# Hybrid DeltaNet/S5 trunk on one core: S5 output products batched by block over the four column groups, states rotated in place, weight ring of four in layer 0

## The chip, the core and the metric

The kernel runs on one core of a Trainium2 chip. A core has TensorE (PE, the matrix array; its weight loads are listed apart as PEld), VectorE (DVE), ScalarE (ACT), GpSimd (POOL) and SyncE (SP), whose queue issues nearly all transfers here. Each engine works through its own queue in order and waits on semaphores for the others. The metric is device time in microseconds of one execution; the median of three runs is used.

## The reference, cut to what matters

The trunk has two layers over 256 tokens of width 1024, all in fp32. Layer 0 is a gated DeltaNet (4 heads) beside an S5 state-space part (32 groups of 16 channels with 64 complex states each), one output projection for both, then a dense SwiGLU. Layer 1 is a differential attention and a top-2-of-8 expert SwiGLU. The change touches the S5 part of layer 0:

```python
_, _, xr, xi = lax.associative_scan(combine, (a_r, a_i, bu_r, bu_i), axis=1)
y = (jnp.einsum('gcn,blgn->blgc', c_re.astype(f32), xr) - jnp.einsum('gcn,blgn->blgc', c_im.astype(f32), xi)
     + d_skip.astype(f32).reshape(S5_GROUPS, S5_GROUP) * u32)
...
ga, gb = jnp.split(y @ glu_w.astype(f32) + glu_b.astype(f32), 2, axis=-1)
```

Each complex state is multiplied by a constant a at every token and takes in bu. The output of a group is the real part of C times the state, plus a skip term.

## The kernel before, in words

**S5.** Two groups (2 x 64 = 128 states) fill the 128 partitions and are called a pair. There are 16 pairs in four blocks of four; a block's outputs are 4 x 32 = 128 channels. `s5_steps` goes through the blocks b and the pairs i. For a pair, two matmuls form bu (L1100). VectorE turns it by tables of cosine and sine, so that the complex recurrence becomes two real scans: products with cos (L1108, tile s5a) and sin (L1109, tile s5b), a sum and a difference in place (L1110, L1111), and two scans over the 256 tokens into z (L1113, tile s5c). The states are then turned back: z times cos on VectorE into a new s5a buffer (L1116) and z times sin on GpSimd into a new s5b buffer (L1117). Four matmuls of 32 columns (L1121) form the pair's 32 outputs in its own 32 partitions of a PSUM bank, py, which is held through the block. After the fourth pair VectorE adds the skip term and writes the outputs over uT (L1123). Each fp32 matmul appears in the profile as two weight loads and two matmuls. s5a, s5b and s5c have two buffers each, in the pool s5tmp. The tables of blocks 0 and 1 are made early by `s5_tables`, those of blocks 2 and 3 inside `s5_steps`; they use s5a and s5b buffers too.

**What sets the order.** `weave` merges four generators by a start and a step for each: the input projection with its convolution (`w_in_steps`), the S5 steps, two DeltaNet lanes (`gdn_steps`), and the sums of the adaLN modulation (`ada`). A program scheduler then orders each engine's queue from this order and its own estimate of times. After the weave come `s5_glu`, which needs all four blocks, and `out_proj`, whose first passes take the S5 halves and the first DeltaNet heads, and whose last pass takes the heads of the second lane.

**Weights.** All large weights come in 1 MB tiles through `raw` (L110): each load waits until a buffer of the ring is free, and the loads stand in one queue on SP. `split` cuts a tile into a high part (L131, ScalarE) and a low part (L132, VectorE), since most products are made of three fp32r matmuls. The ada sums in layer 0 are fp32 matmuls with 32 columns that go over the four column groups in turn (L272). The ring has five buffers in layer 0 (rawp); from the feed-forward on, four more (rawp2) join it, nine in all.

**PSUM.** The tag "ms" has two banks; in the weave they hold bu and py. The tag "gd" has four, for DeltaNet.

Of the kernel before, what the change touches and what calls it, by code (L numbers as in the profile page):

```python
# [9 lines left out]
F32 = mybir.dt.float32  # L10
# [3 lines left out]
ALU = mybir.AluOpType  # L14
# [3 lines left out]
P = 128  # L18
T = 256
# [55 lines left out]
class Trunk:  # L75
# [5 lines left out]
    NM = 2  # L81
    OSP = (0, 1, 2, 3)
    S5B = 2
    WB = 1
    U = (6, 7)

# [74 lines left out]
    def build(self, upto=99):  # L161
        tc, nc, a = self.tc, self.nc, self.a
        ctx = ExitStack()
        with ctx:
            ent = ctx.enter_context
            self.RAW = 2048
            self.WN = 1024
            cpool = ent(tc.tile_pool(name="const", bufs=1))
            self.cp = cpool
            self.sm = ent(tc.tile_pool(name="small", bufs=1))  # L170
            self.wp = ent(tc.tile_pool(name="wsplit", bufs=2))
            self.rawp = ent(tc.tile_pool(name="rawp", bufs=5))
            self.psum = ent(tc.tile_pool(name="psum", bufs=2, space=PSUM))
            self.raws, self.wps = [self.rawp], [self.wp]
            with ExitStack() as c2:
                self.even_layer(upto, c2.enter_context)
            if upto < 4:
                return
            self.wp2 = ent(tc.tile_pool(name="wsplit2", bufs=2))
            self.rawp2 = ent(tc.tile_pool(name="rawp2", bufs=4))  # L180
            self.raws = [self.rawp] * 5 + [self.rawp2] * 4
            self.wps = [self.wp] * 2 + [self.wp2] * 2
            with tc.tile_pool(name="ffn", bufs=1) as self.fp:
                self.scr = self.fp
                self.dense_ffn()
            self.debug("x0", self.x, lambda d: d.rearrange("(t p) n -> p t n", p=P))
            if upto < 5:
                return
            with tc.tile_pool(name="att", bufs=1) as self.ap_:
                self.scr = self.ap_  # L190
                self.diff_attention()
            self.debug("xm1", self.x, lambda d: d.rearrange("(t p) n -> p t n", p=P))
            if upto < 6:
                return
            with tc.tile_pool(name="moe", bufs=1) as self.mp, tc.tile_pool(name="rawp3", bufs=self.R3) as rawp3:
                self.scr = self.mp
                self.raws, self.nraw = self.raws + [rawp3] * self.R3, 0
                self.moe()
# [211 lines left out]
    def even_layer(self, upto, ent):  # L410
        tc, nc, a = self.tc, self.nc, self.a
# [9 lines left out]
        with tc.tile_pool(name="early", bufs=1) as self.prep:  # L421
# [34 lines left out]
            for k2 in range(KD // 2):  # L456
# [3 lines left out]
                with self.behind(self.lastada[:1] if k2 == 2 else ()):  # L460
                    for k in (2 * k2, 2 * k2 + 1):
                        for tt in range(NT):
                            nc.tensor.matmul(pba[:, tt * 8:tt * 8 + 8], hF[:, k, tt * P:(tt + 1) * P], wba[:, k, :],
                                             start=(k == 0 and tt == 0), stop=(k == KD - 1 and tt == 1))
                    for b in range(4):
                        out = pu[b // 2][:, (b % 2) * T:(b % 2 + 1) * T]
                        for kk in range(2):
                            k, o = 2 * k2 + kk, slice(512 * kk + b * P, 512 * kk + b * P + P)
# [7 lines left out]
            with self.behind(self.lastsplit + self.later + [mm.ins]):  # L476
                self.gdn_gates(pba)
        self.gd = ent(tc.tile_pool(name="gdn", bufs=2, reuse_waits="tile"))
        self.yTa = None
        self.qkv = {}  # L480

# [187 lines left out]
    def s5_tables(self, b):  # L669

        nc, V, G = self.nc, self.nc.vector, self.nc.gpsimd
# [2 lines left out]
        cosT = self.tab.tile([P, 4, T], F32, tag="cos", name=self.nm("cos"))  # L674
        sinT = self.tab.tile([P, 4, T], F32, tag="sin", name=self.nm("sin"))
        for h in range(2):
            u = self.tmp.tile([P, 2, T], F32, tag="s5a", name=self.nm("tu"))
            n = self.tmp.tile([P, 2, T], F32, tag="s5b", name=self.nm("tn"))
            for i in range(2):
                r = 4 * b + 2 * h + i  # L680
# [6 lines left out]
            n = self.tmp.tile([P, 2, T], F32, tag="s5b", name=self.nm("tn"))  # L687
# [4 lines left out]
            n = self.tmp.tile([P, 2, T], F32, tag="s5b", name=self.nm("tn"))  # L692
# [392 lines left out]
    def s5_steps(self):  # L1085

        nc, ev, tmp = self.nc, self.ev, self.tmp
        V, G = nc.vector, nc.gpsimd
        crT, ncrT, nciT = self.cT
        for b in range(4):  # L1090
            if b >= 2:
                self.s5_tables(b)
            py = None
            for i in range(4):
                self.mark("s5")
                pr, o = 4 * b + i, 32 * i
# [4 lines left out]
                                     self.uT[o:o + 32, b, :], start=True, stop=True)  # L1101
                pb = pb.rearrange("p (k t) -> p k t", t=T)

                def t2(tag):
                    return tmp.tile([P, 2, T], F32, tag=tag, name=self.nm(tag))

                tcs, tsn, z = t2("s5a"), t2("s5b"), t2("s5c")
                V.tensor_tensor(tcs, pb, cosv, op=ALU.mult)  # L1108
                V.tensor_tensor(tsn, pb, sinv, op=ALU.mult)  # L1109
                V.tensor_tensor(tcs[:, 0, :], tcs[:, 0, :], tsn[:, 1, :], op=ALU.add)  # L1110
# [1 line left out]
                for kind in range(2):  # L1112
                    V.tensor_tensor_scan(z[:, kind, :], self.mag[:, pr:pr + 1].to_broadcast([P, T]), tcs[:, kind, :], 0.0,  # L1113
                                         op0=ALU.mult, op1=ALU.add)
                oc, os_ = t2("s5a"), t2("s5b")
                V.tensor_tensor(oc, z, cosv, op=ALU.mult)  # L1116
                (G if i in self.OSP else V).tensor_tensor(os_, z, sinv, op=ALU.mult)  # L1117
                if py is None:
                    py = self.ps("ms", "py")
                for n, (m, x) in enumerate(((crT, oc[:, 0, :]), (ncrT, os_[:, 1, :]), (nciT, os_[:, 0, :]), (nciT, oc[:, 1, :]))):  # L1120
                    nc.tensor.matmul(py[o:o + 32, :T], m[:, b, o:o + 32], x, start=(n == 0), stop=(n == 3))  # L1121
                yield
            V.scalar_tensor_tensor(self.uT[:, b, :], self.uT[:, b, :], self.colB[:, 48 + b:49 + b], py[:, :T],  # L1123
                                   op0=ALU.mult, op1=ALU.add)


    def dense_ffn(self):
# [709 lines left out]
```

## Time and profile before

| what | value |
|---|---|
| median of three runs | 1378.49 us (1377.51 to 1380.19) |
| the profiled execution | 1378.09 us |
| its span, first to last instruction | 1376.3 us |
| granted TensorE clock, mean | 0.978 |
| S5 steps on VectorE, first to last | 78.9 to 235.2 us |

A row of the busy time by stage gives the stretch, its length, the busy time and instruction count of each engine, the granted clock, the share of time that the DMA engines were busy, and GB/s. With a tile or a line chosen, it counts the instructions of that tile or line alone. A row of waits reads: who waited for whom, microseconds in total, how often, the longest. A row of a group ends in: busy us, mean ns of one, idle time of the engine before them and what ended it. A row of the timeline begins with start and length in microseconds; "x4" is four like instructions merged.

### The profile page before, as it was taken

The numbers are of one execution on the slowest core, as the hardware profiler recorded it, in microseconds if no ns is written. First come the engines' busy times: TensorE is split into PE (matmuls) and PEld (weight loads), VectorE is DVE, ScalarE is ACT, GpSimd is POOL, SyncE is SP. The second block draws the span as 40 slices with busy tenths as digits, with TensorE's granted clock in tenths as the row PEclk, the third lists the DMA queues.
The fourth block names the chain that finished last, engine by engine and source line by source line (L and its number), as shares of the span: only waits on it lengthen the run. The fifth ranks groups of instructions, "written<-read, shape, count | busy, mean of one in ns | idle before, by whom it ended". The sixth has DMA issues, their size and how long they took to land.

```text
span 1376.3 us, 26749 instructions
## 1 busy us (share of the span) xinstructions
PE 1281.9 (93%) x10928; PEld 941.8 (68%) x10928; DVE 826.4 (60%) x1516; ACT 577.1 (42%) x990; POOL 123.6 (9%) x118
## 2 busy tenths in 40 slices
PE   3999999989999978999999999999998899999975
PEld 2777666779999978998788435786352468835334
DVE  6688767567878878965798413986020089820202
ACT  3553322455444444664778213775010168711000
POOL 3132322000000003341100000000000000000000
PEclk9799999999999999999999999999999999999998
DMA  9834334159788967821899899999999999999995
GB/s 262 268 114 132 111 106 154 62 177 325 247 270 287 293 211 252 271 96 63 334 305 399 305 380 409 405 409 356 391 409 405 408 409 406 409 397 408 408 396 208
DMA packets 196164, 400.98 MB, mean 291 GB/s; under 512 B 14797, under 2 KB 115650, under 8 KB 196034
## 3 DMA queue, kind: packets, MB, share of 16 engines
q1 hardware_dynamic: 189610, 398.00, 78.7%
q10 hardware_dynamic: 6424, 1.19, 0.5%
q8 instruction: 88, 1.44, 0.4%
q14 instruction: 42, 0.34, 0.1%
HBM read 398.11 MB, written 1.05 MB: 290 GB/s over the span
## 4 chain that ended last, share of the span: by engine, by line
PE 46%; DMA 10%; DVE 4%; issue 1%; ACT 1%; SPq 1%; POOL 0%; ACTq 0%; DVEq 0%
PE pab L1731 9%; DMA raw<-in_odd_expert_w 9%; PE py L1782 5%; PE pab L1675 4%; PE pab L1674 4%; PE pab L1676 4%; PE py L1708 2%; PE py L1709 2%; PE py L1707 2%; PE px L1625 2%; DVE wlo L132 1%; PE pqk L398 1%; PE pqk L399 1%; PE pqk L400 1%; PE pth L150 1%
## 5 line engine op out<-in xcount | busy, mean ns | idle before, releaser
L131 ACT ACTIVATE whi<-raw 128x1024 fp32r<-128x1024 f32 (+2 forms) x352 | 347.1, 1001 | 279.8 <-PE pab L399 52.3
L132 DVE TENSOR_TENSOR wlo<-raw,whi 128x1024 fp32r<-128x1024 f32 (+2 forms) x352 | 402.9, 1168 | 72.6 <-ACT whi L131 70.6
L1731 PE MATMUL pab<-raw,xg 128*32 128x512 f32 (+1 forms) x1920 | 194.2, 524 | 10.5 <-DMA raw<-in_odd_expert_w 10.5
L1731 PEld LDWEIGHTS pab<-raw,xg 128*32 128x32 f32 x1920 | 58.2, 109 | 118.8 <-issue 77.5
L1751 DVE TENSOR_TENSOR hb<-hb,pab 128x256 f32<-128x256 f32 (+1 forms) x35 | 12.4, 364 | 171.0 <-ACT hb L1750 170.5
L1675 PE MATMUL pab<-wlo,xg 128*128 128x512 f32 (+1 forms) x288 | 110.3, 383 | 3.6 <-DVE wlo L132 3.4
L1676 PE MATMUL pab<-whi,xg 128*128 128x512 f32 (+1 forms) x288 | 106.4, 377 | 0.0
L398 PE MATMUL pab<-hT,whi 128*128 128x256 f32 x352 | 101.9, 290 | 0.0
L399 PE MATMUL pab<-hT,whi 128*128 128x256 f32 x352 | 100.3, 285 | 0.1
L400 PE MATMUL pab<-hT,wlo 128*128 128x256 f32 x352 | 99.9, 284 | 0.0
L1782 PE MATMUL py<-raw,hTe 128*32 128x256 f32 (+1 forms) x1760 | 83.7, 343 | 10.7 <-DMA raw<-in_odd_expert_w 8.6
L282 DVE SCALAR_TENSOR_TENSOR adas<-raw,condr,adas 128x256 f32<-128x256 f32 x175 | 86.4, 499 | 3.1
L1674 PE MATMUL pab<-whi,xg 128*128 128x512 f32 (+1 forms) x288 | 84.4, 379 | 3.6 <-DVE xg L1632 1.9
L1782 PEld LDWEIGHTS py<-raw,hTe 128*32 128x32 f32 x1760 | 53.4, 112 | 38.0 <-DMA raw<-in_odd_expert_w 12.8
L1802 DVE TENSOR_TENSOR yf<-py,gate 32x256 f32<-32x256 f32 (+1 forms) x48 | 18.0, 374 | 102.3 <-PE py L1782 101.3
L1750 ACT ACTIVATE hb<-pab 128x256 f32<-128x256 f32 (+1 forms) x35 | 11.5, 338 | 155.8 <-PE pab L1731 155.1
L399 PEld LDWEIGHTS pab<-hT,whi 128*128 128x128 f32 x352 | 68.0, 193 | 0.8 <-DVE hT L388 0.5
L398 PEld LDWEIGHTS pab<-hT,whi 128*128 128x128 f32 x352 | 68.1, 193 | 0.3
L400 PEld LDWEIGHTS pab<-hT,wlo 128*128 128x128 f32 x352 | 67.9, 193 | 0.1
L1675 PEld LDWEIGHTS pab<-wlo,xg 128*128 128x128 f32 x288 | 54.3, 189 | 19.4 <-DVE wlo L132 6.3
L1676 PEld LDWEIGHTS pab<-whi,xg 128*128 128x128 f32 x288 | 54.4, 189 | 10.0
L1674 PEld LDWEIGHTS pab<-whi,xg 128*128 128x128 f32 x288 | 51.0, 189 | 13.7 <-ACT whi L131 2.2
(465 smaller groups left out, 2504.4 us busy)
## 6 DMA issues: line engine op xcount, KB each, us to landing
raw<-in_odd_expert_w SPq DMA_DIRECT2D x215, 1024.0 KB
raw<-in_ada_w SPq DMA_DIRECT2D x48, 1024.0 KB
raw<-in_odd_expert_w SPq DMA_DIRECT2D x64, 768.0 KB
raw<-in_even_ffn_w SPq DMA_DIRECT2D x33, 1024.0 KB
raw<-in_odd_w_qkv SPq DMA_DIRECT2D x12, 1024.0 KB
raw<-in_even_w_in SPq DMA_DIRECT2D x10, 1024.0 KB
raw<-in_even_w_out SPq DMA_DIRECT2D x4, 1024.0 KB
raw<-in_odd_w_out SPq DMA_DIRECT2D x4, 1024.0 KB
```

What stands on the lines that cost most here:

```text
L131: act = nc.scalar.activation(hs, src, AF.Copy)
L132: dve = nc.vector.tensor_tensor(l, src, hs, op=ALU.subtract)
L282: nc.vector.scalar_tensor_tensor(s, w[:, k, :], self.condr[:, k, 0:1], s, op0=ALU.mult, op1=ALU.add)
L398: nc.tensor.matmul(out, wh[:, o:o + P], hT[:, k, 0, :], start=(k == 0), stop=False)
L399: nc.tensor.matmul(out, wh[:, o:o + P], hT[:, k, 1, :], start=False, stop=False)
L400: nc.tensor.matmul(out, wl[:, o:o + P], hT[:, k, 0, :], start=False, stop=(k == kd - 1))
L1625: PE.matmul(px[:, kk * n:kk * n + n], self.xn[:, tt, k * P:(k + 1) * P], Pt[:, tt, :n], start=(tt == 0), stop=(tt == 1))
L1674: PE.matmul(p[:, :m], xg[:, k, 0, :], wh[:, s], start=(k == 0), stop=False)
L1675: PE.matmul(p[:, :m], xg[:, k, 0, :], wl[:, s], start=False, stop=False)
L1676: PE.matmul(p[:, :m], xg[:, k, 1, :], wh[:, s], start=False, stop=(k == KD - 1))
L1731: PE.matmul(pu[t][32 * g:32 * g + 32], xg[:, k, 32 * t:32 * t + 32], v[:, :, g * n:(g + 1) * n], start=(k == 0 and (t == 0 or n > P)), sto ...
L1782: PE.matmul(py[32 * g:32 * g + 32, t], hs[f][t], v[:, i, g * n:(g + 1) * n], start=(f == 0 and t == 0), stop=(f == NF - 1 and t == 1))
```

## The change

The four pairs of a block are first all scanned and rotated back; then 16 matmuls form the block's outputs together, product by product, and within a product pair by pair, so that successive matmuls go to the four column groups in turn. The bank py is taken only then. The rotated states stay in place: z times cos overwrites the pair's s5a buffer, z times sin overwrites z. s5a (five buffers) and s5c (four) move to a new pool, s5out, opened after the early pool is closed; s5b keeps its two. The tables of blocks 0 and 1 get buffers of their own in the early pool. The weight ring has four buffers in layer 0, and five join it afterwards, nine in all as before.

```diff
+    S5O = (5, 4)
...
-            self.rawp = ent(tc.tile_pool(name="rawp", bufs=5))
+            self.rawp = ent(tc.tile_pool(name="rawp", bufs=4))
...
-            self.rawp2 = ent(tc.tile_pool(name="rawp2", bufs=4))
-            self.raws = [self.rawp] * 5 + [self.rawp2] * 4
+            self.rawp2 = ent(tc.tile_pool(name="rawp2", bufs=5))
+            self.raws = [self.rawp] * 4 + [self.rawp2] * 5
...
+        self.s5o = ent(tc.tile_pool(name="s5out", bufs=1))
...
-            u = self.tmp.tile([P, 2, T], F32, tag="s5a", name=self.nm("tu"))
+            if b < 2:
+                u = self.prep.tile([P, 2, T], F32, tag="tu", name=self.nm("tu"), bufs=2)
+            else:
+                u = self.s5o.tile([P, 2, T], F32, tag="s5a", name=self.nm("tu"), bufs=self.S5O[0])
...
-            py = None
+            outs = []
...
-                tcs, tsn, z = t2("s5a"), t2("s5b"), t2("s5c")
+                tcs, tsn, z = t2("s5a", self.s5o, self.S5O[0]), t2("s5b", tmp, 2), t2("s5c", self.s5o, self.S5O[1])
...
-                oc, os_ = t2("s5a"), t2("s5b")
-                V.tensor_tensor(oc, z, cosv, op=ALU.mult)
-                (G if i in self.OSP else V).tensor_tensor(os_, z, sinv, op=ALU.mult)
-                if py is None:
-                    py = self.ps("ms", "py")
-                for n, (m, x) in enumerate(((crT, oc[:, 0, :]), (ncrT, os_[:, 1, :]), (nciT, os_[:, 0, :]), (nciT, oc[:, 1, :]))):
-                    nc.tensor.matmul(py[o:o + 32, :T], m[:, b, o:o + 32], x, start=(n == 0), stop=(n == 3))
-                yield
+
+                V.tensor_tensor(tcs, z, cosv, op=ALU.mult)
+                (G if i in self.OSP else V).tensor_tensor(z, z, sinv, op=ALU.mult)
+                outs.append((tcs, z))
+                if i < 3:
+                    yield
+
+            py = self.ps("ms", "py")
+            for n, (m, k, x) in enumerate(((crT, 0, 0), (ncrT, 1, 1), (nciT, 1, 0), (nciT, 0, 1))):
+                for i in range(4):
+                    o = 32 * i
+                    nc.tensor.matmul(py[o:o + 32, :T], m[:, b, o:o + 32], outs[i][k][:, x, :], start=(n == 0), stop=(n == 3))
             V.scalar_tensor_tensor(self.uT[:, b, :], self.uT[:, b, :], self.colB[:, 48 + b:49 + b], py[:, :T],
                                    op0=ALU.mult, op1=ALU.add)
+            yield
```

More of the change, by code (lines that the diff above doesn't have):

```diff
@@ L1102, in s5_steps, with t2 @@
                 pb = pb.rearrange("p (k t) -> p k t", t=T)
-                def t2(tag):
-                    return tmp.tile([P, 2, T], F32, tag=tag, name=self.nm(tag))
-                tcs, tsn, z = t2("s5a"), t2("s5b"), t2("s5c")
+                def t2(tag, pool, bufs):
+                    return pool.tile([P, 2, T], F32, tag=tag, name=self.nm(tag), bufs=bufs)
+                tcs, tsn, z = t2("s5a", self.s5o, self.S5O[0]), t2("s5b", tmp, 2), t2("s5c", self.s5o, self.S5O[1])
                 V.tensor_tensor(tcs, pb, cosv, op=ALU.mult)
```

## The prediction

> **What bounds the kernel now.** I read the page, then the busy time by stage, then the waits of the stage that holds the S5 work.
>
> ```profile
> span 1376.3 us, 26749 instructions
> PE 1281.9 (93%) x10928; PEld 941.8 (68%) x10928; DVE 826.4 (60%) x1516; ACT 577.1 (42%) x990; POOL 123.6 (9%) x118
> ```
>
> ```profile
> core 0: us, PE busy (x) PEld busy (x) DVE busy (x) ACT busy (x) POOL busy (x), PEclk, DMA share, GB/s
> 75.00:237.00 162.00, 158.59 (x1414) 112.64 (x1412) 126.73 (x251) 54.91 (x111) 44.89 (x36) 0.98 0.38 125
> 237.00:300.00 63.00, 58.99 (x456) 49.64 (x456) 34.38 (x74) 26.11 (x64) 2.67 (x4) 1.00 0.22 74
> ```
>
> The edited code runs in the first of these stretches, 75 to 237 us, where four lanes are woven together. TensorE shows 158.6 of 162 us busy, VectorE 126.7 (78%), and the DMA engines 0.38 of their time. The second stretch (GLU, rest of the DeltaNet lanes, output projection) has TensorE at 59.0 of 63. So time taken off TensorE up to 237 us has work behind it to pull forward, as far as about 300 us. A busy TensorE row alone proves little, since ends of matmuls are modelled; the waits say the same:
>
> ```profile
> PE py L1121 <- DVE s5a L1116: 1.1, 1, 1.1
> PE prow L897 <- POOL rn L158: 0.9, 1, 0.9
> PE pqkv L398 <- DVE cacc L840: 0.7, 1, 0.7
> PE gvb L297 <- ACT adas L277: 0.6, 1, 0.6
> ```
>
> ```profile
> DVE s5a L1116 <- PE py L1121: 6.5, 4, 2.1
> DVE uT L1123 <- PE py L1121: 6.5, 4, 2.5
> DVE s5a L1108 <- PE bu L1100: 3.9, 4, 2.4
> ```
>
> The first four rows are all that TensorE's matmuls waited for in the stretch: 3.3 us. VectorE waits for TensorE, 17 us in these three rows alone. TensorE is the bound here.
>
> **The change, part by part.** *The output matmuls (L1121).* Each pair's output is four fp32 products with 32 output columns, recorded as eight matmuls in one column group. The kernel has a second user of the same shape, the ada matmuls of L272, which are issued over the four column groups in turn, as the new batch will be:
>
> ```profile
> L1121 PE MATMUL py<-s5b,ncT 128*32 128x256 f32 x64 | 17.6, 400 | 0.0
> L272 PE MATMUL gv<-raw,condr 128*32 128x256 f32 x192 | 17.3, 390 | 0.0
> ```
>
> ```profile
> 75.00:237.00 162.00, 34.28 (x128) 12.08 (x128) 1.92 (x4) 0.98 0.38 125
> 75.00:237.00 162.00, 17.34 (x192) 6.08 (x192) 0.98 0.38 125
> ```
>
> ```profile
> 123.06 1.07 PE L272 MATMUL gv<-raw,condr 128*32 128x256 f32 x16
> 124.06 1.13 PE L1100 MATMUL bu<-uT,wb 32*128 32x256 f32 x4
> ```
>
> The second fence is the busy time of the tile py (128 matmuls, 34.28 us) and of L272 (192 matmuls, 17.34 us). One record lasts the same in both (400 and 390 ns), but a py record costs 34.28/128 = 268 ns of TensorE and an ada record 17.34/192 = 90 ns, because four of them run side by side. At the ada price the new 128 records cost 128 x 0.090 = 11.6 us, so 34.28 - 11.56 = 22.7 us go. The batches are twice as long (32 records, the ada ones 16), and 16 records take 124.06 - 123.06 = 1.00 us until the next work starts; with one closing tail of about 0.34 us a batch of 32 would take 2.0 + 0.34 = 2.34 us, four of them 9.4 us, so at most 24.9 us go. I take 22.7.
>
> ```profile
> L272 PEld LDWEIGHTS gv<-raw,condr x192: 105/109/178, 123.1 to 225.8; 128*32 128x32 f32 x192
> ```
>
> A rule speaks against this. The Trainium skill, "TensorE: Matmul & The Clock Gate", Part 3, "The mechanism", says that a weight load overlaps matmuls in flight only where the row group differs; column groups share their row group. By it a batch could not hide its 32 loads and the gain would be near 0 instead of 22.7 us. The trace disagrees: the 192 loads of L272 are 109 ns each, 20.9 us in sum, and occupy 6.08 us of the row above. I keep the row.
>
> *The rotated states in place (L1116, L1117).* Instruction counts and sizes on VectorE and GpSimd do not change. Two orders do. VectorE no longer needs a fresh s5a buffer for z*cos, so its 6.5 us of waiting for py (L1116, above) go. GpSimd now writes z where VectorE has just read it, so its product starts after L1116 and not beside it.
>
> ```profile
> L1116 DVE TENSOR_TENSOR s5a<-s5c,cos 128x512 f32<-128x512 f32 x16 | 15.1, 946 | 7.0 <-PE py L1121 6.5
> L1108 DVE TENSOR_TENSOR s5a<-bu,cos 128x512 f32<-128x512 f32 x16 | 10.9, 684 | 4.0 <-PE bu L1100 3.9
> L1109 DVE TENSOR_TENSOR s5b<-bu,sin 128x512 f32<-128x512 f32 x16 | 10.9, 680 | 0.0
> L1110 DVE TENSOR_TENSOR s5a<-s5a,s5b 128x256 f32<-128x256 f32 x16 | 6.8, 428 | 0.2
> ```
>
> ```profile
> L1117 POOL TENSOR_TENSOR s5b<-s5c,sin 128x512 f32<-128x512 f32 x16 | 24.6, 1536 | 80.2 <-DVE s5c L1113 62.7 <-PE ptr L150 7.3 <-PE gv L272 6.5
> ```
>
> ```profile
> 82.56 1.73 POOL L1117 TENSOR_TENSOR s5b<-s5c,sin 128x512 f32<-128x512 f32 x1 [7.93 <-DVE s5c L1113]
> ```
>
> ```profile
> 83.33 2.04 DVE L132 TENSOR_TENSOR wlo<-raw,whi 128x1024 fp32r<-128x1024 f32 x1 [0.20 <-ACT whi L131]
> 46.72 1.22 DVE L132 TENSOR_TENSOR wlo<-raw,whi 128x1024 fp32r<-128x1024 f32 x1
> ```
>
> L1116 takes 946 ns in the mean where the like-sized L1108 takes 684: it sometimes meets GpSimd. After the change the clash is not gone but lands on whatever VectorE does next; the split at 83.33 us, met by GpSimd's product of 82.56 to 84.29, took 2.04 us where the undisturbed one took 1.22. Bounds: 16 x (946 - 684) = 4.2 us of VectorE time won if no later instruction is hit, and 16 x 0.82 - 4.2 = 8.9 us lost if each product hits a split. I take 0, since clashes occur now at both places.
>
> The Trainium skill, "SBUF — State Buffer", section "SBUF: two separate sides", calls this an exclusive lock between GpSimd and a VectorE operation with two SBUF inputs, the later one waiting out the earlier. The two rows agree: 84.29 + 1.22 is 85.5 us, and the split ended at 85.37. By the rule alone the worst case would be each product blocking VectorE for its whole 1.54 us.
>
> *The join at a block's end.* The batch waits for the fourth pair's GpSimd product, and the next block's first scan needs a z buffer that only the batch frees (four z buffers, four pairs). On VectorE that scan and what is queued behind it (splits, convolution, DeltaNet steps) can stand. The chain is L1116 0.68, then GpSimd 1.54, then the batch 2.34: 4.6 us, of which the next pair's first steps (L1108 and L1109, 1.36 us, and two half-size steps as L1110, 0.86 us) cover 2.2, since a fifth s5a buffer is there. That leaves 2.4 us at each of three joins, 7 us, with other lanes' VectorE and TensorE work to fill it; bounds 0 and 7, I take 3. Tables of blocks 2 and 3 draw on the same five buffers and lie in the same gaps. At the last block 2.34 us of batch replaces 8 x 0.268 = 2.1 us: nothing.
>
> *One matmul bank.* py now occupies one of the two "ms" PSUM buffers for a batch, not for a whole block, so bu of the next pair can run ahead: part of the 3.9 us of L1108. No credit beyond the terms above.
>
> *VectorE nears its own bound.* If the stretch shrinks to 162 - 22.7 = 139.3 us, VectorE's 126.7 us fill 91% of it. The feed-forward stage shows the two side by side that full:
>
> ```profile
> 420.00:440.00 20.00, 20.00 (x148) 19.02 (x147) 17.91 (x34) 7.51 (x10) 0.00 (x0) 1.00 0.92 295
> ```
>
> There VectorE is at 90% and TensorE does not idle. That code is more regular than this stretch; loss between 0 and 8 us, I take 3.
>
> *Ring of four in layer 0, five in the second pool.* Every load of layer 0 goes one freed slot later.
>
> ```profile
> 258.51 0.37 SPq L110 DMA_DIRECT2D raw<-in_even_ffn_w  x1
> ```
>
> ```profile
> 291.45 10.40 SPq L110 DMA_DIRECT2D raw<-in_even_ffn_w  x5
> ```
>
> ```profile
> SPq L110 <- DVE wlo L132: 64.6, 4, 32.5
> ```
>
> ```profile
> 278.48 1.06 ACT L131 ACTIVATE whi<-raw 128x1024 fp32r<-128x1024 f32 x1 [3.98 <-PE po L718]
> ```
>
> ```profile
> 300.41 1.04 ACT L131 ACTIVATE whi<-raw 128x1024 fp32r<-128x1024 f32 x1
> 308.39 1.05 ACT L131 ACTIVATE whi<-raw 128x1024 fp32r<-128x1024 f32 x1
> ```
>
> ```profile
> 300.00:420.00 120.00, 117.37 (x818) 110.85 (x819) 96.74 (x156) 59.72 (x85) 4.87 (x6) 0.97 0.87 292
> ```
>
> The queue of SP does stand for slots here (64.6 us, held by splits). The third output-projection load would go near 257 us and is first split at 278.5: hidden, with 20 us of cover. The first feed-forward load moves from 258.5 to the slot freed at 291.4, and its split stands at 300.4: 9 us of cover for one megabyte, which at 292 GB/s takes 3.6 us. The feed-forward loads behind it come one megabyte, 3.6 us, later; the second split at 308.4 still has its data, and the stage after has DMA at 0.87 with TensorE full. Bounds 0 and 3.6, I take 1.5. Without the cover it would be the whole 3.6. Earlier in the layer there is more cover:
>
> ```profile
> 78.10 22.01 SPq L110 DMA_DIRECT2D raw<-in_ada_w  x3
> ```
>
> These three ada loads go between 78.1 and 100.1 us, and the first of them is read at 123.06 (L272, above), so one slot later, 9 us or so, costs 0. Later stages keep nine buffers: 0.
>
> *New pool.* The pool of s5a and z lies where the early pool was and may wait for its last reader, the gate matmul L809:
>
> ```profile
> L809 PE MATMUL pd<-r,cst x4: 592/592/697, 72.5 to 78.7; 128*128 128x512 f32 x4
> L1108 DVE TENSOR_TENSOR s5a<-bu,cos x16: 677/684/692, 78.9 to 224.8; 128x512 f32<-128x512 f32 x16
> ```
>
> It ends at 78.7 + 0.6 = 79.3, the first S5 step starts at 78.9; 0 or 0.4, I take 0.5 with its wait.
>
> **The sum**, against the profiled execution: 1378.1 - 22.7 + 3 (joins) + 3 (VectorE) + 1.5 (ring) + 0.5 (pool) = 1363.4 us. That execution was timed at 1378.09 us around a span of 1376.3; the median of the runs is 1378.49, 0.4 above, so 1363.8.
>
> **Rivals.** *VectorE takes over as the bound.* With every product hitting a split (+8.9 us) VectorE needs 135.6 us. Of its 162 - 126.7 = 35.3 idle us 17 end with TensorE (the three rows of waits); if the other 18.3 stay, the stretch takes 153.9 us: 8.1 won, 1370.4. For it: 78% already, with chains in every lane. Against: most of its named waits are for TensorE.
>
> *Nothing is won.* The busy row of TensorE hides slack (the weight loads fill only 112.6 of 162 us) and the DeltaNet chain, which also runs to the output projection, sets the end; or the batch does not overlap. Then 1378.5. Against: the four rows of waits, and L272.
>
> *Slower: the join serialises S5.* One block's end costs the whole chain: L1116, GpSimd, a batch queued in order behind other lanes' matmuls (2.5 us, the longest wait for py above), the batch itself, about 7.1 us, four times 28 us, with the tables behind it. If nothing fills this, the stretch grows by 28 - 22.7 = 5 us: 1383.5. It decides from 22.7/4 = 5.7 us of uncovered wait at a join. For it: GDN, S5 and ada were spread by weave steps that fit the old costs. Against: the first steps of the next pair are free of the join, and TensorE has other lanes to run.
>
> **How the numbers follow.** Forecast (8 to 25 us won) 0.70; VectorE 0.10; nothing 0.09; slower 0.11. Low end: the best price without losses, 1378.5 - 24.9 = 1353.6, rounded 1354. High end 1376: it takes in the VectorE rival and leaves out the other two, 0.20. About 0.2%, 2.7 us, is what a measurement can tell from no change; so faster 0.80, same 0.09, slower 0.11.
>
> **What would show it.** Right: py's busy time near 10 to 12 us instead of 34.28; TensorE still over 95% busy in the S5 stretch; the uT update of the last block some 15 us earlier than 234.7; VectorE's waits of L1116 gone.
>
> ```profile
> 234.73 0.48 DVE L1123 SCALAR_TENSOR_TENSOR uT<-uT,colB,py 128x256 f32<-128x256 f32 x1 [1.68 <-PE py L1121]
> ```
>
> Wrong: TensorE rows that wait for s5c products of GpSimd at block ends; VectorE over 95% busy with TensorE idle; a first feed-forward split that waits for its load; or S5 ending early while the output projection still ends near 300 us because DeltaNet does.

## The result, and the profile after

The changed kernel is slower: 1396.14 us (median of four runs, 1393.09 to 1398.92) against 1378.76 (1377.51 to 1380.19, with a fourth run beside the three above), a ratio of 1.0124 with a 95% interval of 1.0098 to 1.0149. That is 17 us lost where 15 won were forecast, and outside the range. The profiled execution took 1397.9 us around a span of 1395.8. Medians here and below are over all executions of a kernel, while ratios leave out slow ones (1828 us at a clock of 0.647 in e1_ring4, 1662 at 0.709 in e11_two, 1405 at 0.950 in e7_half).

The stretch of the edited code, and in it the tile py, in the busy time by stage of the changed kernel (columns as before):

```profile
75.00:237.00 162.00, 142.73 (x1289) 106.71 (x1287) 127.08 (x239) 52.38 (x105) 42.99 (x37) 0.88 0.33 108
```

```profile
75.00:237.00 162.00, 20.07 (x128) 5.66 (x128) 1.89 (x4) 0.88 0.33 108
```

TensorE is busy for 142.7 of the 162 us (158.6 before), VectorE as long as before (127.1 and 126.7), and the granted clock has gone from 0.98 to 0.88. py costs 20.07 us instead of 34.28. So work did leave TensorE, and nothing came forward into the space. TensorE's waits in that stretch, the longest groups:

```profile
PE prow L902 <- POOL rn L159: 5.3, 2, 4.7
PE pkk L918 <- DVE qkvs L904: 3.1, 1, 3.1
PE pqkv L399 <- DVE cacc L845: 3.0, 2, 1.8
PE py L1131 <- DVE s5a L1121: 2.2, 4, 0.7
```

The waits are for DeltaNet's norm (rn), its convolution (cacc) and what follows them (qkvs). The batch itself waits for little (the row of py, and 0.8 us more for GpSimd's products). S5 is not late; its last update of uT starts 4 us earlier than the 234.73 of before:

```profile
230.68 0.48 DVE L1132 SCALAR_TENSOR_TENSOR uT<-uT,colB,py 128x256 f32<-128x256 f32 x1 [2.20 <-PE py L1131]
```

Late is DeltaNet. Its input projections (the last of their three matmul lines; first and last start in us), before and after:

```profile
L400 PE MATMUL pqkv<-hT,wlo x96: 276/282/416, 67.3 to 145.4; 128*128 128x256 f32 x96
```

```profile
L401 PE MATMUL pqkv<-hT,wlo x96: 276/282/416, 67.8 to 158.9; 128*128 128x256 f32 x96
```

They end 13.5 us later. The residual sums at the end of the output projection, before and after, are as late:

```profile
L734 DVE TENSOR_TENSOR x<-x,res x8: 414/422/426, 293.7 to 299.3; 128x256 f32<-128x256 f32 x8
```

```profile
L739 DVE TENSOR_TENSOR x<-x,res x8: 414/416/417, 306.5 to 312.1; 128x256 f32<-128x256 f32 x8
```

So 12.8 us are lost by x. The other 6.7 us between the two profiled executions lie behind it (1376.3 - 299.7 = 1076.6 us from x to the end before, 1083.3 after), in code that the change doesn't touch. Among the variants below this part takes 1075.5 to 1087.0 us and goes with no one edit, so it is not explained here.

**Where the 12.8 us went.** The busy time from 75 us to x, before and after:

```profile
75.00:300.00 225.00, 217.58 (x1870) 162.28 (x1868) 161.12 (x324) 81.02 (x174) 47.55 (x40) 0.98 0.33 110
```

```profile
75.00:313.00 238.00, 213.12 (x1874) 164.49 (x1872) 163.96 (x324) 81.19 (x174) 45.66 (x41) 0.91 0.32 106
```

Each length is idle time, plus busy time lost to a low clock, plus work at full clock. Before: 225 - 217.6 = 7.4 idle, 217.6 x 0.02 = 4.4 lost to the clock, 213.2 of work. After: 24.9 idle, 213.1 x 0.09 = 19.2 lost, 193.9 of work. (The last two are estimates: the clock is given to 0.01, and its mean over the stretch is applied to the busy time. The half-speed stretches themselves, 6.8 us before and 41.0 after, hold 6.7 and 33.1 us of busy time, and half of that is 3.4 and 16.6. So these terms are good to about 3 us.) The work fell by 18 to 19 us, which is near the 22.7 of the forecast. Idle time rose by 17.5, and the clock took 13 to 15 more. 17.5 + 14.8 - 19.3 = 13.0, the difference of the two lengths.

**Where it starts.** VectorE's queue in the first block, before:

```profile
83.33 2.04 DVE L132 TENSOR_TENSOR wlo<-raw,whi 128x1024 fp32r<-128x1024 f32 x1 [0.20 <-ACT whi L131]
85.30 0.99 DVE L840 SCALAR_TENSOR_TENSOR cacc<-pqkv,colB,cacc 128x255 f32<-128x255 f32 x2
86.20 1.21 DVE L132 TENSOR_TENSOR wlo<-raw,whi 128x1024 fp32r<-128x1024 f32 x1
87.33 0.47 DVE L840 SCALAR_TENSOR_TENSOR cacc<-pqkv,colB,cacc 128x253 f32<-128x253 f32 x1
```

and after:

```profile
85.52 0.48 DVE L845 SCALAR_TENSOR_TENSOR cacc<-pqkv,colB,cacc 128x255 f32<-128x255 f32 x1
85.92 0.68 DVE L1113 TENSOR_TENSOR s5a<-bu,cos 128x512 f32<-128x512 f32 x1
86.52 0.68 DVE L1114 TENSOR_TENSOR s5b<-bu,sin 128x512 f32<-128x512 f32 x1
87.11 0.47 DVE L845 SCALAR_TENSOR_TENSOR cacc<-pqkv,colB,cacc 128x254 f32<-128x254 f32 x1
87.50 0.68 DVE L1113 TENSOR_TENSOR s5a<-bu,cos 128x512 f32<-128x512 f32 x1
88.10 0.68 DVE L1114 TENSOR_TENSOR s5b<-bu,sin 128x512 f32<-128x512 f32 x1
...
90.50 0.86 DVE L845 SCALAR_TENSOR_TENSOR cacc<-pqkv,colB,cacc 128x255 f32<-128x255 f32 x2
```

The convolution takes three steps of cacc for each projected tile. Before, they stand together (85.30 to 87.8, with one split between). After, the first products of S5's second and third pair stand between them, and the tile is done at 91.4: 5.8 us instead of 2.5. (The next tile of before is mixed with S5's steps too and takes 3.1 us. Over the whole stretch it is ScalarE's wait for the convolution that tells, 11.6 us before and 36.8 after, in rows further down.) TensorE's next projection waits for the tile:

```profile
91.51 0.55 PE L399 MATMUL pqkv<-hT,whi 128*128 128x256 f32 x1 [1.75 <-DVE cacc L845]
91.86 0.41 PE L400 MATMUL pqkv<-hT,whi 128*128 128x256 f32 x1
```

In the next microseconds the projections' matmuls last 0.41 us where they lasted 0.28. The clock by slices of 3.4 us of the changed kernel shows it:

```profile
85.70:89.10 3.40, 3.18 (x17) 2.23 (x17) 3.40 (x7) 1.21 (x2) 1.27 (x1) 0.99 0.01 2
89.10:92.50 3.40, 1.65 (x7) 1.02 (x5) 3.40 (x8) 0.42 (x1) 0.00 (x0) 0.50 0.39 118
92.50:95.90 3.40, 3.40 (x17) 3.40 (x17) 3.40 (x8) 0.00 (x0) 0.00 (x0) 0.50 0.54 191
```

Two slices run at half clock, the second with TensorE fully busy. VectorE is full in all three, and at 95.9 us the clock is full again. The clock falls at 89.1 us, before the wait of 1.75 us, which begins at 89.8. In the slice ahead of the fall TensorE's rows are busy for 3.18 us, but from 85.5 on with small matmuls alone: S5's input products (32 rows of the array), sums with one column and the first output products (32 columns). Half speed comes six more times before x.

### The profile page after: what moved, and what is told of

Its sections match the earlier page's. It is cut to its first block, busy times and chain, and to the rows that moved or that the text cites. A ratio compares the mean times of both kernels' runs of the same rounds, so it can differ in the third digit from the quotient of the medians.

```text
span 1395.8 us, 26742 instructions
## 1 busy us (share of the span) xinstructions
PE 1280.6 (92%) x10928; PEld 947.1 (68%) x10928; DVE 829.4 (59%) x1516; ACT 578.0 (41%) x990; POOL 119.1 (9%) x118
## 4 chain that ended last, share of the span: by engine, by line
PE 48%; DMA 8%; DVE 4%; issue 1%; ACT 1%; POOL 1%; ACTq 0%; DVEq 0%; POOLq 0%
PE pab L1741 9%; DMA raw<-in_odd_expert_w 7%; PE py L1792 5%; PE pab L1685 4%; PE pab L1684 4%; PE pab L1686 4%; PE py L1718 2%; PE px L1635 2%; PE py L1719 2%; PE py L1717 2%; PE pqk L399 1%; PE pqk L400 1%; DVE yf L1812 1%; PE pqk L401 1%; DVE wlo L133 1%
## 5 line engine op out<-in xcount | busy, mean ns | idle before, releaser
L1685 PEld LDWEIGHTS pab<-wlo,xg 128*128 128x128 f32 x288 | 54.4, 189 | 19.5 <-DVE wlo L133 5.5
```

The source lines that it names most:

```text
L1685: PE.matmul(p[:, :m], xg[:, k, 0, :], wl[:, s], start=False, stop=False)
```

## The experiments

Ratios are to the kernel before on the same chip, with 95% intervals. Different builds of one arithmetic differ by some microseconds through the order that the scheduler finds, and one profiled execution can lie up to 9 us from its kernel's median (e16_conv40: 1388.94 and 1379.90). So verdicts go by ratios, and the profile serves to say where.

**First round: which part of the change.** *e1_ring4*: the kernel before with the weight ring of four and five alone.

> The kernel before with only the weight rings changed (four buffers in layer 0, five after it). Theory A (S5 steps, freed from waiting for TensorE, fill VectorE's queue early, and TensorE idles at 75 to 175 us, with its clock at half after each gap): the ring alone is worth 0 to 3 us, 1378 to 1382. Theory B (later loads are what leaves TensorE without work): most of the 17 us, 1390 or more.

1385.22 us, ratio 1.0038 [1.0014, 1.0062]: 2 to 9 us lost by itself, more than theory A allowed and far from theory B.

*e2_pairs*: the changed kernel with each pair's outputs formed in the pair's own step.

```diff
...
-                outs.append((tcs, z))
+                if py is None:
+                    py = self.ps("ms", "py")
+                for n, (m, x) in enumerate(((crT, tcs[:, 0, :]), (ncrT, z[:, 1, :]), (nciT, z[:, 0, :]), (nciT, tcs[:, 1, :]))):
+                    nc.tensor.matmul(py[o:o + 32, :T], m[:, b, o:o + 32], x, start=(n == 0), stop=(n == 3))
...
```

> The changed kernel with one edit taken back: each pair's four output products follow the pair at once, in one column group, as before; in place, buffers (5 and 4) and ring as changed. Theory A: the buffers let S5 run ahead just as much and TensorE has 22 us more work, so 1395 or more, with VectorE over 90% busy at 75 to 175 us. Theory C (the batch, issued in bits, does the harm): about 1379 to 1382.

1381.93, 1.0016 [1.0002, 1.003]. Ring, buffers and states in place together cost about 2 us. The harm comes with the batch (or with the bank that it frees and the new order, which this run doesn't tell apart), and larger buffers alone do none.

*e3_inplace*: the kernel before with the states in place alone (two buffers each, ring of five; the new pool and the tables' own buffers stay).

> The kernel before with the rotated states kept in place and nothing else: two buffers each for s5a and z, products pair by pair, ring of five. GpSimd's product now starts after VectorE's. Theory A: S5 is held back by its two buffers as before, so 1376 to 1382 and no long TensorE gaps. Theory D (GpSimd's later start holds up the DeltaNet norms queued behind it): 1385 or more, with gaps of TensorE ended by the norms on GpSimd.

1383.86, 1.0023 [1.0008, 1.0038]: some 3 us, between the ranges of the two theories.

*e4_batch*: the changed kernel with the 16 output matmuls queued behind the fourth pair's input products.

```diff
...
+                    with self.behind([bu.ins]):
+                      nc.tensor.matmul(py[o:o + 32, :T], m[:, b, o:o + 32], outs[i][k][:, x, :], start=(n == 0), stop=(n == 3))
```

> The changed kernel with the 16 output matmuls of a block held behind the fourth pair's bu, so that they can't be issued in bits. Theory A: TensorE's time for py falls from 20 to about 12 us, but VectorE's order stays, so 1388 to 1398. Theory C: near 1365 to 1380.

1398.11, 1.0114 [1.0097, 1.0131]: unchanged. The edit moved less than it was meant to. In its trace the first of these matmuls still starts at 91.4 us, 22 us ahead of the block's update at 113.3, since the fourth pair's input products are themselves done by then. So it doesn't tell whether a batch that is issued in bits costs anything. On every engine its other instructions up to x come in the order of the changed kernel.

**Second round: work or place.** *e5_serial*: the changed kernel with the batch's two loops exchanged, so that a pair's four products go to one column group in succession.

```diff
-            for n, (m, k, x) in enumerate(...):
-                for i in range(4):
+            for i in range(4):
+                for n, (m, k, x) in enumerate(...):
```

> The changed kernel, its 16 output matmuls still together at the end of the block and all buffers as they are, but pair by pair (the four products of one column group in succession, so about 268 ns each instead of 90). It puts the removed TensorE time (some 14 to 23 us) back at the batch's place. Theory F (filler: from 75 to 175 us VectorE is the bound, the output matmuls were what TensorE did meanwhile, and without them it idles and its clock goes to half): near the kernel before, 1378 to 1385. Theory J (join: the place at the end of the block, with sums and products held until then, does the harm) and theory K (bank: the output's PSUM bank, no longer held through the block, lets S5 run ahead on VectorE): as slow as the changed kernel or slower by the work put back, 1396 to 1410.

1378.28, 0.9978 [0.9951, 1.0005]. With the removed TensorE time put back, the loss is gone. That fits F. But the scheduler also found another order (S5's last update starts at 215.2 us, 15.5 earlier), so order and work are not yet apart.

*e6_hold*: the changed kernel with the bank of py asked for at the start of the block.

> The changed kernel with the output's PSUM bank taken at the start of the block (before the first pair's input products) instead of at its end, so that the input products have one of the two banks again. Theory K: the harm is gone, 1365 to 1382, and VectorE's cacc waits are back near 12 us. Theories F and J: no change, 1393 to 1400.

1398.36, 1.0131 [1.0078, 1.0185]. This tests nothing. The trace shows the input products of the first block's four pairs done by 86.3 us, run ahead as after: the bank is taken at the first write to it, and that had not moved. The order on every engine is that of the changed kernel, so this is a second measurement of it. The last run takes the bank properly.

*e7_half*: the pair-by-pair variant without two of the four output products.

> The pair-by-pair variant (outputs formed in each pair's step, buffers, states in place and ring as changed; 1382 before) with two of the four output products of each pair left out, so that its output is not the reference's: some 17 us of TensorE work gone and nothing else moved. Theory F: TensorE idles instead, the clock shows half-speed stretches between 75 and 200 us, and the time is 1382 to 1398. Theories J and K: the work was on the path, 1362 to 1370.

1395.61, 1.0099 [1.0065, 1.0134]. Removing TensorE work made it 1% slower, with no batch, no join and nothing else moved in the source. The scheduler's order did move, though (S5's last update starts at 245.4 us, in e2_pairs at 230.9), so order and work are not apart here either; and the profiled execution, at 1403.27 us, lies 8 above the median. Busy time from 75 us to its x:

```profile
75.00:314.00 239.00, 224.24 (x1817) 169.14 (x1815) 162.56 (x325) 82.00 (x172) 46.28 (x41) 0.89 0.32 105
```

Here it is the clock above all: 224.2 x 0.11 = 24.7 us.

*e8_late*: the changed kernel with S5's step in the weave raised from 3.8 to 4.6.

> The changed kernel with S5's step in the hand-written order raised from 3.8 to 4.6, so that S5's pairs rank later against DeltaNet's work. Theory O (order: S5's pairs and tables pass ahead of DeltaNet's convolution and norms on VectorE and GpSimd, and TensorE then starves): 1375 to 1390, with fewer half-speed stretches. Theory F: no gain, 1393 to 1402.

1388.08, 1.0062 [1.0035, 1.0089]: some 8 us won, yet the last projection starts as late as after (159.4 us), so the gain is not where theory O put it.

**Third round: the order held.** In the next two, issue-order edges on every engine pin all instructions but the output matmuls to the order of another variant. The edges ask for order alone, not for a wait.

```diff
+    for e, idx in order.items():
+        for p, q in zip(idx, idx[1:]):
+            tc.add_manual_dep(per[e][q], per[e][p].name,
+                              mybir.DependencyInfo(mybir.DependencyClass.NoSync, mybir.DependencyReason.DATA), reason="pin")
```

*e9_pin*: outputs of two pairs at a time, pinned to the order of e2_pairs. (Four at a time was not built in that order; the buffers were judged too few for it.)

> Outputs of two pairs at a time formed together (two column groups in turn, after the second and the fourth pair), buffers, states in place and ring as changed, and the order of all other instructions on every engine pinned to that of the pair-by-pair variant (1382 before) by issue-order edges. TensorE work goes away (some 10 to 17 us) while nothing else changes place. Theory P (plan: TensorE's work was worth its time, but the planner, which lays down each engine's order from its own model, found a worse order once the output products moved): 1364 to 1378. Theory F (filler: TensorE idles instead and its clock halves, whatever the order): 1382 to 1397, with more half-speed stretches between 75 and 200 us.

1386.02, 1.0039 [1.0017, 1.0062], against 1.0016 [1.0002, 1.003] for e2_pairs. *e10_serial*: e4_batch with the loops exchanged as in e5_serial, pinned to the order of e4_batch.

> The variant with the 16 output matmuls queued behind the fourth pair's input products (1398 before), these matmuls pair by pair (268 ns each instead of 90), and the order of all other instructions on every engine pinned to that variant's own. Some 11 us of TensorE work is put back and nothing else changes place. Theory P: as slow or slower by the work, 1398 to 1410. Theory F: the work fills TensorE's gaps and keeps its clock up, 1378 to 1390.

1389.30, 1.0065 [1.0041, 1.009], against 1.0114 [1.0097, 1.0131]: faster. The tile py from 75 to 235 us, and TensorE from 75 us to x, of e4_batch and then of e10_serial:

```profile
75.00:235.00 160.00, 18.99 (x128) 5.51 (x128) 1.89 (x4) 0.89 0.33 107
75.00:317.00 242.00, 217.06 (x1889) 168.27 (x1888) 165.62 (x328) 82.03 (x174) 47.79 (x42) 0.91 0.33 107
```

```profile
75.00:235.00 160.00, 30.58 (x128) 12.22 (x128) 1.88 (x4) 0.95 0.35 113
75.00:309.00 234.00, 216.26 (x1884) 164.55 (x1882) 163.78 (x326) 82.03 (x173) 46.93 (x42) 0.96 0.33 108
```

Eleven more microseconds of TensorE work in an order that is otherwise the same end 8 us sooner: the idle time falls from 24.9 to 17.7 us and the loss to the clock from 19.5 to 8.7. So a missing piece of TensorE work cost more than its own length here. That is theory F with the order out of the way. The two traces also say where. By S5's last update (231.8 and 229.3 us) e10_serial is 2.5 us ahead, 1.0 of them from before 75 us; so in the S5 stretch itself the extra work costs nothing. Some 5 us more come behind it, where e4_batch has two half-speed stretches (6.8 us from 238.8 and 3.4 from 266.1) and e10_serial none. Apart from the matmuls, the instructions last equally long in both (VectorE's from 75 us to x 185.2 and 184.7 us in sum). With the order held, then, it is the clock that makes less work end later.

The other side is weaker: in e2_pairs' order the removal of some 8 us of py's busy time changed the ratio by 0.0023, with intervals that overlap. It shows that nothing was won, and not how much was lost. Since e10_serial keeps some 9 us of loss with all of the work back, F is not the whole cause.

*e11_two*: as e9_pin, with the order left to the scheduler.

> As the first of these, two pairs at a time, with the order left to the planner. Theory F: TensorE's work goes away as in the first, 1382 to 1397, near it. Theory P: a different time from the first by more than 5 us, to either side.

1393.95, 1.0095 [1.0064, 1.0125]: 8 us above the same work in the pinned order. Order matters as much as work.

**Fourth round: what passes what.** *e12_conv*: the changed kernel with the lane of the input projections and their convolution under high priority.

```diff
-        self.weave((0, w[0], self.w_in_steps(hT)), ...
+        self.weave((0, w[0], self.ahead(self.w_in_steps(hT), 200)), ...
```

> The changed kernel with the lane of DeltaNet's input projections and convolution put under high priority (an offset of 200), so that its convolution steps go ahead of S5's products on VectorE when both are ready. Theory V (VectorE's order: S5's pairs, run ahead through the freed bank and the larger buffers, pass the convolution that TensorE waits for): 1378 to 1390, the last projection near 150 us instead of 159. Theory F alone (too little TensorE work beside a full VectorE): 1393 to 1400.

1376.62, 0.9974 [0.9949, 1.0]: 20 us won over the changed kernel, a little under theory V's range, with the last projection starting at 152.6 us. Its busy time from 75 us to x, and its first convolution steps on VectorE:

```profile
75.00:298.00 223.00, 205.50 (x1875) 162.96 (x1873) 162.41 (x324) 84.67 (x175) 49.76 (x41) 0.92 0.35 112
```

```profile
84.40 0.48 DVE L845 SCALAR_TENSOR_TENSOR cacc<-pqkv,colB,cacc 128x255 f32<-128x255 f32 x1
84.80 0.68 DVE L1113 TENSOR_TENSOR s5a<-bu,cos 128x512 f32<-128x512 f32 x1
85.39 0.68 DVE L1114 TENSOR_TENSOR s5b<-bu,sin 128x512 f32<-128x512 f32 x1
85.99 0.47 DVE L845 SCALAR_TENSOR_TENSOR cacc<-pqkv,colB,cacc 128x254 f32<-128x254 f32 x1
...
87.05 0.47 DVE L845 SCALAR_TENSOR_TENSOR cacc<-pqkv,colB,cacc 128x253 f32<-128x253 f32 x1
```

The tile is done at 87.5 instead of 91.4. ScalarE's wait for the convolution (75 to 300 us), before, after and here:

```profile
ACT qkvs L842 <- DVE cacc L840: 11.6, 4, 4.5
```

```profile
ACT qkvs L847 <- DVE cacc L845: 36.8, 6, 8.3
```

```profile
ACT qkvs L847 <- DVE cacc L845: 24.0, 7, 8.5
```

Still, against the kernel before, this version has some 24 us less TensorE work up to x, 10 more of idle time and 12 more lost to the clock: by the same estimate, 17.5 idle, 16.4 lost and 189.1 us of work in its 223.

*e16_conv40*: the same with an offset of 40.

> The changed kernel with the convolution lane's priority offset 40 instead of 200. Theory V: within 6 us of the 1377 with 200. If that was a lucky order: 1388 to 1400.

1379.90, 0.9999 [0.9972, 1.0026]: confirmed. *e15_beforeconv*: the same priority in the kernel before.

> The kernel before with the lane of DeltaNet's projections and convolution under the same high priority (offset 200). Theory V (the priority undoes what the change did to VectorE's order): no gain here, 1376 to 1390, since the convolution is not passed by S5 in this kernel. Were the priority a gain of its own: 1355 to 1368.

1385.08, 1.0045 [1.0021, 1.0069]: no gain there. So the priority undoes what the change did, and is no improvement of its own. *e17_serialconv*: e5_serial with the priority.

> The changed kernel with its output matmuls pair by pair (1378) and the convolution lane under priority 200. If the batch earns TensorE time once the convolution goes first: slower than 1377 by 5 to 15 us, 1382 to 1392. Theory F (less TensorE work has no worth beside a full VectorE): 1372 to 1380, the same or under it.

1383.28, 1.0033 [1.0011, 1.0054]: by the ratios of e12_conv and e16_conv40 the batch now earns 5 to 8 us, as the first of the two forecasts had it. That is about half of what it takes off TensorE (py from 75 to 235 us is 29.54 us here and 14.89 in e12_conv), and the order is another one here too.

*e13_convlate*: e12_conv with S5's lane starting at 10 and stepping by 4.6. *e14_beforelate*: the kernel before with the step of 4.6.

> As the run before, and S5's lane starts at 10 instead of 4 and steps by 4.6 instead of 3.8. Theory V: 1370 to 1385, under the first. Theory F alone: 1388 to 1400.

> The kernel before with S5's step raised from 3.8 to 4.6. If the gain that this brought the changed kernel (1398 to 1388) is its own, by theory V: 1377 to 1386, no gain. If the slower pace is simply better: 1366 to 1374.

1384.36, 1.0025 [0.9988, 1.0061], a miss, not under e12_conv but 8 us above it, though the intervals touch; and 1386.13, 1.0055 [1.0027, 1.0084], so a slower pace is no gain in general. The steps of the weave are a fine setting in each version.

*e18_bank*: the changed kernel with py's bank really taken at the start of the block.

```diff
+            py = self.ps("ms", "py")
+            nc.tensor.matmul(py[0:32, T:T + 8], crT[:, b, 0:32], self.uT[:, b, 0:8], start=True, stop=True)
...
-            py = self.ps("ms", "py")
```

> The changed kernel with the output's PSUM bank really taken at the start of the block: a matmul of 8 columns into a part of the bank that nothing reads, ahead of the first pair's input products (four such matmuls in all, under 1 us together). Theory K (the freed bank lets S5's input products, and with them its VectorE work, pass the convolution): 1370 to 1386, the input products of the first block spread past 95 us as in the kernel before. If the buffers or the batch itself do it: 1392 to 1400.

1385.67, 1.0049 [1.0027, 1.0071]: 10 of the 17 us come back, at the upper edge of what theory K allowed. The first and the last of the four pairs' input products in the first block, before, after and here:

```profile
77.15 1.12 PE L1100 MATMUL bu<-uT,wb 32*128 32x256 f32 x4
...
97.35 1.12 PE L1100 MATMUL bu<-uT,wb 32*128 32x256 f32 x4
```

```profile
77.59 1.13 PE L1105 MATMUL bu<-uT,wb 32*128 32x256 f32 x4
...
87.53 1.13 PE L1105 MATMUL bu<-uT,wb 32*128 32x256 f32 x4
```

```profile
79.59 1.12 PE L1107 MATMUL bu<-uT,wb 32*128 32x256 f32 x4
...
98.33 1.13 PE L1107 MATMUL bu<-uT,wb 32*128 32x256 f32 x4
```

With one bank, a pair's input products had to wait until VectorE had read those of the pair before. With two, all four pairs are offered to VectorE by 88.7 us, ten microseconds sooner, and their products stand between the steps of the convolution. With the bank held, the last projection ends at 144.9 us (before: 145.8), and ScalarE waits 22.4 us for the convolution instead of 36.8. TensorE's own waits for it are not shorter (4.0 us, 3.0 after). The scheduler planned this version anew, and two orders of the same work differed by 8 us above, so how much of the 10 us belongs to the bank alone is not shown.

## Why the prediction was wrong, point by point

**The price of the matmuls: right in kind, short in size.** The term of 22.7 us stands against 14.2 of busy time (34.28 - 20.07). The prediction took the batch for one run of 32 records; in the trace its products go out as their pairs are ready, the first at 88.9 us and the update at 111, and products that go alone overlap less. Besides, 7.0 of the 20.07 us lie in half-speed stretches. In e12_conv, where more of the products go together and 1.1 us of them lie at half speed, py costs 14.89 us between 75 and 235. That the 32 loads would hide, against the rule of the Trainium skill that the prediction cites, held: the 128 loads occupy 5.66 us in the row of py.

**"So time taken off TensorE up to 237 us has work behind it to pull forward": the step that failed.** It was read from a TensorE at 158.6 of 162 us and from waits of 3.3 us in sum. These show that TensorE was fed, by this order and with this much to do. They don't show that its next work would have been ready any earlier. The projections wait for a PSUM bank that the convolution on VectorE must empty, and DeltaNet's norms for GpSimd. With VectorE at 78% over the whole stretch and 84% from 75 to 175 us, little can come forward. e9_pin and e10_serial show it with the order held: some 8 us of output work taken away won nothing, and 11 us put back ended 8 us sooner. e7_half points the same way in an order of its own.

```profile
75.00:175.00 100.00, 97.70 (x698) 71.49 (x697) 84.20 (x155) 37.98 (x72) 29.07 (x25) 0.97 0.36 117
```

```profile
75.00:175.00 100.00, 82.18 (x569) 63.92 (x568) 92.06 (x163) 35.33 (x67) 33.32 (x29) 0.85 0.29 93
```

Before and after, from 75 to 175 us: VectorE goes from 84 to 92 us, TensorE from 98 to 82.

**"VectorE nears its own bound", 3 us, bounds 0 and 8.** The term was named and mis-sized, by evidence of the wrong kind. The feed-forward row (VectorE at 90%, TensorE never idle) is a stage of one regular chain that runs ahead by its buffers. In the weave four chains cross, and the idle time rose by 17.5 us. The VectorE rival had the right engine, with a chance of 0.10 and a time 6.6 us above the forecast; it still expected 8 us won, because it priced VectorE's throughput and not the place of one chain in its queue.

**"No credit beyond the terms above", for the freed bank: wrong in sign.** Bu did run ahead, as that sentence said. What was not asked is what the run-ahead passes: the queue of VectorE holds the convolution that TensorE waits for. e18_bank puts up to 10 us on it, in an order of its own, and e12_conv and e16_conv40 bring back all 17 by giving the convolution its place again.

**The clock: not priced.** It stood at 0.98 in the row that was quoted, and was taken for granted. It cost some 13 to 15 us more after, nearly as much as the idle time. No variant changes the clock alone, but the executions of one program do: the ten of e13_convlate go from 1373.5 us at a mean clock of 0.971 to 1393.7 at 0.952, in step with it. 0.019 of 1384 us is 26, and 20 lie between them. So most of what the clock takes seems to arrive at the end of the kernel, as it did between e4_batch and e10_serial.

**The slower rival: right side, wrong mechanism.** It had S5 serialised at the joins. TensorE's waits for the batch's inputs are 2.2 us in the row above and 0.8 for GpSimd's products, and S5 ended 4 us earlier. The chance of 0.11 for all that is slower was too small, since it was carried by this one mechanism. Nearest in mechanism was the rival that nothing is won (0.09): slack under a busy row, and DeltaNet's chain setting the end. It put no price on TensorE losing its clock. Of the signs of being wrong, the last one came: S5 ended early while DeltaNet kept the output projection late.

**States in place and ring.** VectorE's waits for py at L1116 are gone, as said (0.0 in the row of L1121). Its instructions are hit elsewhere. Scans before, then scans, z times cos and the sum after (60 to 330 us; busy, mean ns, idle before):

```profile
L1113 DVE TENSOR_TENSOR_SCAN s5c<-mag,s5a 128x256 f32<-128x256 f32 x32 | 20.5, 676 | 0.0
```

```profile
L1118 DVE TENSOR_TENSOR_SCAN s5c<-mag,s5a 128x256 f32<-128x256 f32 x32 | 24.3, 794 | 1.1 <-PE py L1131 1.1
L1121 DVE TENSOR_TENSOR s5a<-s5c,cos 128x512 f32<-128x512 f32 x16 | 13.7, 857 | 0.0
L1115 DVE TENSOR_TENSOR s5a<-s5a,s5b 128x256 f32<-128x256 f32 x16 | 8.5, 532 | 0.1
```

That is 3.8 - 1.4 + 1.7 = 4.1 us more of VectorE time on these lines, inside the bounds of 4.2 won and 8.9 lost, where 0 was taken. By themselves, states in place cost about 3 us (e3_inplace) and the ring about 5 (e1_ring4, with 1.5 taken and 3.6 as the upper bound; in its profile 4.0 of 4.3 us lie behind x); together with the buffers they cost 2 (e2_pairs). These are not additive, and each is about as large as what another order of the same work does.

**What stays open.** e5_serial runs ahead as the changed kernel does (its four input products start by 86.0 us) and is as fast as the kernel before; the scheduler found it another order from about 100 us on. Which detail of that order saves it was not found. Nor was the four-wide batch tried in that order, which would tell whether the order alone carries the loss.

## What to carry to other kernels

A busy engine shows that it is fed, not that it would be fed sooner: before taking work off it, ask which chain makes its next work ready, and how full that chain's engine is. When an edit frees a bank or a buffer, list what may now run ahead and what it will pass in each in-order queue; if that is what the busiest engine waits for, give the latter priority in the same edit. Here the batch with that priority (1376.6 us, ratio 0.9974 [0.9949, 1.0]) is level with the kernel before, or a few microseconds under it (0.9999 with the other offset).

## What the runs showed of the hardware

TensorE's clock halves within a busy stretch, in steps of 3.4 us. The records of the granted clock show half-speed stretches of 3.4 and 6.8 us between 75 us and x, 6.8 us in all before and 41 after; a projection matmul then takes 410 ns instead of 280. The Trainium skill, "TensorE: Matmul & The Clock Gate", Part 1, "What's actually happening", has this clock follow how busy TensorE has been, in windows of 3.4 us, and the lengths agree. Its section "HAM oscillation — how this bites in real kernels" puts the danger at idle gaps above 3.4 us. Here the longest wait of the whole stretch is 4.7 us. Of the seven half-speed stretches after, three stand beside waits of 1.8 to 4.7 us (those from 89.1, 126.6 and 164.1), two beside waits under 0.9 us (from 106.1 and 150.5) and two beside none (from 191.5 and 239.2). Ahead of these two, TensorE's rows are busy for 6.8 us on end, but the last 3.4 of them hold only matmuls that use 64 rows or 64 columns of the array (L918, L935, L989, L995). The second stretch of before (171.8 us) has no wait beside it either, and matmuls of 32 to 64 rows or columns in the 3.4 us ahead. So a busy row is no proof against half speed, and the limit of 3.4 us does not hold here. Not every such window brings it: in e10_serial the same matmuls, from 233.2 to 237.5 us, were followed by full clock.

Nor is a hole always punished; in the kernel before, with the slice after the hole:

```profile
147.90:151.30 3.40, 1.89 (x21) 0.82 (x20) 3.40 (x9) 0.77 (x2) 2.64 (x4) 1.00 0.28 67
151.30:154.70 3.40, 3.40 (x29) 3.40 (x30) 2.63 (x4) 0.00 (x0) 2.84 (x3) 1.00 1.09 369
```

TensorE was idle for 1.5 of 3.4 us and kept its clock. What exactly sets it off is not settled by these runs.
